# A diffusion step with SSD and differential attention on one core: prompt weights transposed in the other small PSUM bank, an output tile begun early, score blocks spaced anew

## The chip, the cores and the metric

One core of one Trainium2 chip. The metric is the device time of one execution in microseconds. The kernel before takes 1878.71 us, the median of three runs (1876.8 to 1879.6).

## What is computed

One inference step of a backbone with two layers. Layer 0 mixes tokens with a bidirectional Mamba-2 scan, layer 1 with differential attention; behind each stands a gated feed-forward part with a convolution of width 3. There are 128 context ("prompt") tokens and 512 latent tokens, the model is 1024 wide, and attention has 8 heads with two key maps of 64 each. The change touches attention and its output projection alone:

```python
def diff_attend(q, k, v, lam):
    ...
        s = jnp.einsum('bqhcd,bkhcd->bhcqk', qi, k, preferred_element_type=F32) * DA_SCALE
        p = jax.nn.softmax(s, axis=-1)
        w = p[:, :, 0] - lam * p[:, :, 1]
        return jnp.einsum('bhqk,bkhd->bqhd', w.astype(v.dtype), v)
...
def diff_out(o, subln_g, out_w, lam_init):
    b, l = o.shape[:2]
    o = (_rms(o) * subln_g.astype(F32) * (1.0 - lam_init)).astype(o.dtype)
    return o.reshape(b, l, D_MODEL) @ out_w
...
            op = diff_out(diff_attend(qp, kp, vp, lam), att_subln_g[slot], att_out_w[slot], lam_init)
            ...
            k_all = jnp.concatenate([cache_k[:, slot], ks_], axis=1)
            v_all = jnp.concatenate([cache_v[:, slot], vs], axis=1)
            os_ = diff_out(diff_attend(qs, k_all, v_all, lam), att_subln_g[slot], att_out_w[slot], lam_init)
```

Prompt tokens attend to prompt tokens. Latent tokens attend to 640 keys: 512 latent ones and 128 from the cache.

## The kernel before

Everything is float32 by three products: each operand is split into a high part and the rest (names ending in h and l, `whi` and `wlo` for weights), and a product is hi by hi, hi by lo and lo by hi. A **dense tile** is 128 output rows for all 640 tokens. Its 8 steps over the input (`dense_many`, L158) have six matmuls each, 256 and 384 columns for each of the three products. After each step comes `hook` (L76), which counts a **tick**. It also advances the generator tasks that are due: a task that says `yield n` gets its next turn n ticks later, and `drain` runs a task to its end. So the order in which the work is written down comes from the waits in these generators. A scheduler then sets the order on each engine from it, by what each instruction needs.

Attention (`attention`, L1169) makes for each head the tiles q, k and v. Beside them run these tasks. A head's prompt scores lie in its own v; its four score blocks and its tail lie beside the tiles of the next two heads:

- `att_head` (L1068): the prompt's scores (`sp`), then four blocks of 128 latent queries. A block's scores are two accumulators (`sl`), one for each key map. The vector engine takes the row maximum (`TENSOR_REDUCE`), the scalar engine the exponential `e` with its row sum, and both combine the two maps to the weights `w` (the prompt's are `wp`).
- `att_tail` (L1123): transposes the prompt's weights (`wpt`, copied to `wpT`), then, for five chunks of 128 keys, transposes four blocks of weights (`wt`), splits them on the scalar (`wTh`) and the vector engine (`wTl`) and multiplies by the values (`ov`, three matmuls). Then `op` for the prompt, the mean square (`osq`, `ms`), a reciprocal root in nine small steps on the vector engine (`rs_v`, `rs_a`, `rs_y`, L178 and following), and the scaling of `o`. Heads 0 to 6 spread the root over the partitions by way of DRAM (`rsd`, `rbc`), head 7 by matmuls (`obc`).
- `att_v` (L999): splits v and transposes it (`vt`).

Behind head 7's v come the output tiles (`po`): `project_out` (L282) multiplies heads 0 to 5 into tiles 0 to 4, and `project_last` (L290) adds heads 6 and 7 to these and makes tiles 5 to 7 from all eight heads, first for columns A (256 tokens), then B (384). `gate_add` adds a tile to the residual `xr`.

PSUM: dense tiles, `sp` and each `sl` take one of three slots of two banks. Two single banks remain. Bank "m" serves `vt`, `wt`, `wpt`, `op` and `ms` in turn, bank "y" serves `ov` and the norms' spreading. Weights are loaded and cast by units (`prefetch`, `cast`, `nextw`): `whi` by the scalar engine, `wlo` by the vector engine, three buffers each, so that the cast of a unit waits for the last use of the one three before.

## Time and profile before

| | |
|---|---|
| median of three runs | 1878.71 us |
| the profiled execution, its own time | 1880.65 us |
| its span | 1878.9 us |
| tensor engine busy | 98% of the span |
| vector engine busy | 73% |
| scalar engine busy | 51% |
| HBM | 111 GB/s |

The profile comes from one execution with the hardware profiler. Its span runs from the first to the last instruction; the execution's own time has 1.75 us more around it. Times in the trace count from the start of the span. Attention's heads with their tails lie between 1052 and 1353, the rest of the output projection up to 1400. PE is the tensor engine's matmuls, PEld its weight loads, DVE the vector and ACT the scalar engine. A wait is idle time of an engine, put down to the instruction whose end came last.

### The profile page before, as it was taken

The numbers are of one execution on the slowest core, as the hardware profiler recorded it, in microseconds if no ns is written. First come the engines' busy times: TensorE is split into PE (matmuls) and PEld (weight loads), VectorE is DVE, ScalarE is ACT, GpSimd is POOL, SyncE is SP. The second block draws the span as 40 slices with busy tenths as digits, with TensorE's granted clock in tenths as the row PEclk, the third lists the DMA queues.
The fourth block names the chain that finished last, engine by engine and source line by source line (L and its number), as shares of the span: only waits on it lengthen the run. The fifth ranks groups of instructions, "written<-read, shape, count | busy, mean of one in ns | idle before, by whom it ended". The sixth has DMA issues, their size and how long they took to land.

```text
span 1878.9 us, 32832 instructions
## 1 busy us (share of the span) xinstructions
PE 1838.2 (98%) x13322; PEld 1741.9 (93%) x13322; DVE 1369.5 (73%) x2637; ACT 952.9 (51%) x1745; POOL 0.2 (0%) x4
## 2 busy tenths in 40 slices
PE   7999999999999999999999999999999999999997
PEld 5899999999999999999999988888899999999996
DVE  5699999999658999974555877788777543553554
ACT  3489687878336441441443656566445432431441
POOL 0000000000000000000000000000000000000000
PEclk9999999999999999999999999999999999999998
DMA  9835243436624556532222212111122222122211
GB/s 337 266 121 147 97 147 109 140 115 202 199 80 142 185 180 221 181 103 91 68 68 78 79 40 65 58 50 48 61 88 89 69 79 80 63 72 89 64 40 57
DMA packets 79679, 209.74 MB, mean 112 GB/s; under 512 B 9276, under 2 KB 16040, under 8 KB 79400
## 3 DMA queue, kind: packets, MB, share of 16 engines
q1 hardware_dynamic: 78952, 207.13, 33.5%
q8 instruction: 104, 1.70, 0.4%
q10 hardware_dynamic: 576, 0.52, 0.1%
q14 instruction: 47, 0.39, 0.1%
HBM read 201.66 MB, written 5.96 MB: 111 GB/s over the span
## 4 chain that ended last, share of the span: by engine, by line
PE 91%; DVE 4%; ACT 3%; DMA 1%; issue 1%; SPq 0%; DVEq 0%; ACTq 0%
PE up L104 31%; PE po L104 25%; PE z L104 6%; PE x L104 5%; PE st L104 5%; PE bc L104 3%; PE yp L104 3%; PE q L104 2%; PE v L104 2%; PE k L104 1%; PE modrow L104 1%; PE sl L104 1%; PE in L104 1%; ACT whi L95 1%; ACT e L95 1%; PE ov L104 1%
## 5 line engine op out<-in xcount | busy, mean ns | idle before, releaser
L95 ACT ACTIVATE whi<-raw 128x1024 fp32r<-128x1024 f32 (+3 forms) x227 | 234.2, 1033 | 387.2 <-PE po L104 239.6
L101 DVE TENSOR_TENSOR wlo<-raw,whi 128x1024 fp32r<-128x1024 f32 (+2 forms) x226 | 269.2, 1192 | 172.2 <-ACT whi L95 165.1
L98 DVE SCALAR_TENSOR_TENSOR xr<-po,mod,xr 128x256 f32<-128x256 f32 (+2 forms) x231 | 89.2, 433 | 162.0 <-PE po L104 161.8
L104 PE MATMUL po<-mh,whi 128*128 128x256 f32 (+1 forms) x704 | 167.8, 310 | 0.0
L104 PE MATMUL po<-ml,whi 128*128 128x256 f32 (+1 forms) x704 | 167.5, 310 | 0.0
L104 PE MATMUL po<-mh,wlo 128*128 128x256 f32 (+1 forms) x704 | 167.3, 310 | 0.0
L104 PE MATMUL up<-h11h,wlo 128*128 128x256 f32 (+1 forms) x656 | 149.4, 309 | 0.0
L104 PE MATMUL up<-h01h,wlo 128*128 128x256 f32 (+1 forms) x656 | 149.4, 308 | 0.0
L104 PE MATMUL up<-h01h,whi 128*128 128x256 f32 (+1 forms) x656 | 149.3, 308 | 0.0
L104 PE MATMUL up<-h01l,whi 128*128 128x256 f32 (+1 forms) x656 | 149.3, 308 | 0.0
L104 PE MATMUL up<-h11l,whi 128*128 128x256 f32 (+1 forms) x656 | 149.3, 308 | 0.0
L104 PE MATMUL up<-h11h,whi 128*128 128x256 f32 (+1 forms) x656 | 149.3, 308 | 0.0
L104 PEld LDWEIGHTS po<-mh,whi 128*128 128x128 f32 x704 | 128.5, 188 | 0.7 <-ACT mh L95 0.5
L104 PEld LDWEIGHTS po<-mh,wlo 128*128 128x128 f32 x704 | 128.8, 188 | 0.0
L104 PEld LDWEIGHTS po<-ml,whi 128*128 128x128 f32 x704 | 128.6, 188 | 0.0
L104 PEld LDWEIGHTS up<-h01h,whi 128*128 128x128 f32 x656 | 119.3, 188 | 0.0
L104 PEld LDWEIGHTS up<-h01h,wlo 128*128 128x128 f32 x656 | 119.3, 188 | 0.0
L104 PEld LDWEIGHTS up<-h01l,whi 128*128 128x128 f32 x656 | 119.3, 188 | 0.0
L104 PEld LDWEIGHTS up<-h11h,whi 128*128 128x128 f32 x656 | 119.2, 188 | 0.0
L104 PEld LDWEIGHTS up<-h11h,wlo 128*128 128x128 f32 x656 | 119.2, 188 | 0.1
L104 PEld LDWEIGHTS up<-h11l,whi 128*128 128x128 f32 x656 | 119.2, 188 | 0.0
L98 DVE SCALAR_TENSOR_TENSOR ca<-uraw,fcw,ca 128x511 f32<-128x511 f32 (+1 forms) x176 | 85.2, 546 | 11.6 <-ACT ca L95 11.6
(497 smaller groups left out, 4315.6 us busy)
## 6 DMA issues: line engine op xcount, KB each, us to landing
raw<-in_w_up SPq DMA_DIRECT2D x88, 512.0 KB, 3.5
mw<-in_modT SPq DMA_DIRECT2D x48, 512.0 KB, 3.5
raw<-in_w_in SPq DMA_DIRECT2D x40, 512.0 KB, 5.5
rb<-rowd SPq DMA_DIRECT2D x40, 512.0 KB, 5.6
raw<-in_w_dn SPq DMA_DIRECT2D x32, 448.0 KB, 3.2
raw<-in_w_qkv SPq DMA_DIRECT2D x24, 512.0 KB, 3.5
mr<-in_mod SPq DMA_DIRECT2D x44, 256.0 KB, 5.7
mp<-in_modp SPq DMA_DIRECT2D x32, 256.0 KB, 5.4
```

What stands on the lines that cost most here:

```text
L95: return self.nc.scalar.activation(out, in_, func, **k)
L98: return self.nc.vector.scalar_tensor_tensor(out, in0, s, in1, op0, op1)
L101: return self.nc.vector.tensor_tensor(out, a, b, op)
L104: return self.nc.tensor.matmul(out, lhsT, rhs, start=start, stop=stop)
```

## The change

1. `dense_many`: a part of a tile's steps can be made alone (the last step is counted from `i0`).
2. `project_out` casts, at its last tile, one more unit of weights.
3. `project_last`: heads 0 to 5 of tile 5, columns A (18 matmuls) are made first, ahead of what heads 6 and 7 add to tiles 0 to 4; in the tile's old place only heads 6 and 7 are left (6 matmuls).
4. `weight_units`: the unit of tile 5 comes before the units with the weights of heads 6 and 7.
5. `att_head`: other waits between the prompt's scores and the four blocks, and between the blocks of heads 0 and 1; the task starts three ticks earlier for heads 1 to 6. In dense matmuls from one block to the next, the steady heads had 45, 27, 36 and 36, and have 39, 33, 36 and 36.
6. `att_tail`: `wpt` goes to bank "y"; the last key chunk waits three ticks, not two (head 7 stays at one).

```diff
--- before.py
+++ after.py
@@ -158,7 +158,7 @@
     def dense_many(self, tiles, ks, h, parts, n=None, i0=0):
 
 
-        n = n or len(ks)
+        n = n or i0 + len(ks)
         for i, k in enumerate(ks, i0):
             for ps, (hi, lo), m in tiles:
                 st, sp = i == 0, i == n - 1
@@ -279,11 +279,14 @@
         for a, b, c in COND[half]:
             self.stt(self.x[i][:, a:b], ps[:, COL0[half] + a:COL0[half] + b], g[:, i, c:c + 1], self.x[i][:, a:b], ALU.mult, ALU.add)
 
-    def project_out(self, h, ks, g, tiles=range(KT)):
+    def project_out(self, h, ks, g, tiles=range(KT), ahead=0):
 
         for i in tiles:
             ps = self.dense_ps("po")
-            self.dense(ps, self.nextw(), ks, h)
+            w = self.nextw()
+            if i == tiles[-1]:
+                self.cast(self.wi + ahead)
+            self.dense(ps, w, ks, h)
             for hf in "AB":
                 self.gate_add(i, ps, g, hf)
 
@@ -291,6 +294,8 @@
 
 
         self.norm_begin()
+        first = [(self.dense_ps("po"), self.nextw(), P)] if ks_last else []
+        self.dense_many(first, range(ks[0]), h, "A", KT)
         for i in range(KT - 3):
             ps = self.dense_ps("po")
             n = len(ks) * P
@@ -301,13 +306,14 @@
             for hf in "AB":
                 self.gate_add(i, ps, g, hf)
                 self.norm_sq(i, hf)
-        ks = ks_last or ks
+        ks_from, ks = ks[0], ks_last or ks
         if self.modtask:
             self.drain(self.modtask)
-        ws = [(self.dense_ps("po"), self.nextw(), i) for i in range(KT - 3, KT)]
+        ws = [(*(first[i] if i < len(first) else (self.dense_ps("po"), self.nextw()))[:2], KT - 3 + i) for i in range(3)]
         for hf in parts:
             for grp in ((ws[0:1], ws[1:3]) if hf == "B" else (ws[0:1], ws[1:2], ws[2:3])):
-                self.dense_many([(ps, w, P) for ps, w, i in grp], ks, h, hf)
+                i0 = ks_from if first and hf == "A" and grp == ws[0:1] else 0
+                self.dense_many([(ps, w, P) for ps, w, i in grp], ks[i0:], h, hf, i0=i0)
                 for ps, w, i in grp:
                     self.gate_add(i, ps, g, hf)
                     self.norm_sq(i, hf)
@@ -1098,7 +1104,7 @@
         last = hd == 7
         w = pool.tile([P, TP], F32, tag="wp", name="wp", bufs=1)
         combine(w, TP, *em, st)
-        yield 3 if last else 5 if hd else 3
+        yield {0: 3, 1: 13, 7: 3}.get(hd, 8)
         ws = []
         for b in range(4):
             qb = slice(b * P, (b + 1) * P)
@@ -1117,14 +1123,14 @@
             combine(wb, T, *em, st)
             ws.append(wb)
             if b < 3:
-                yield {0: (3, 2, 2), 6: (2, 2, 2), 7: (1, 1, 1)}.get(hd, (4, 4, 4))[b]
+                yield {0: (2, 3, 5), 1: (3, 3, 3), 6: (2, 2, 2), 7: (1, 1, 1)}.get(hd, (4, 4, 4))[b]
         self.tails[hd] = self.add(self.att_tail(hd, w, ws, vs, o, pool), 1 if last else 4)
 
     def att_tail(self, hd, w, ws, vs, os_, pool):
 
         nc = self.nc
         vh, vl, vp = vs
-        pm = self.bank("m", "wpt")
+        pm = self.bank("y", "wpt")
         nc.tensor.transpose(pm[:, :P], w, self.ident)
         wpT = pool.tile([P, TP], F32, tag="wpT", name="wpT", bufs=1)
         self.act(wpT, pm[:, :P], AF.Copy)
@@ -1150,7 +1156,7 @@
             if prev:
                 av(kc - 1, *prev)
             prev = hi, lo, gate
-            yield 1 if hd == 7 else 2
+            yield 1 if hd == 7 else 2 if kc < NCH - 1 else 3
         av(NCH - 1, *prev)
         self.act(o[:, :TS], py, AF.Copy)
         pm = self.psm.tile([P, 512], F32, tag="m", name="op")
@@ -1182,7 +1188,7 @@
             q = self.att_q(q, hd, pool)
             k = self.att_k(k, hd, pool)
             vs = []
-            tk.append(self.add(self.att_head(hd, qp, kp, q, k, vs, o, pool), 1 if hd == 7 else 4))
+            tk.append(self.add(self.att_head(hd, qp, kp, q, k, vs, o, pool), 1 if hd else 4))
             self.add(self.att_v(self.next_tile(h, "v"), hd, vs, pool), 1)
             if hd:
                 self.drain(tk[hd - 1])
@@ -1190,7 +1196,7 @@
         for i in range(n0):
             self.drain(self.tails[i])
         hy = [self.split(o[i], f"o{i}") for i in range(n0)]
-        self.project_out(hy, range(n0), self.gate(1, 0), range(KT - 3))
+        self.project_out(hy, range(n0), self.gate(1, 0), range(KT - 3), 1)
         self.drain(tk[7])
         for t in self.tails.values():
             self.drain(t)
@@ -1239,7 +1245,8 @@
         per = 1024 // (D - c)
         u += [(a["w_ao"][i:j, :, c:].rearrange("i p c -> p i c"), (j - i) * (D - c))
               for i in range(0, KT - 3, per) for j in (min(i + per, KT - 3),)]
-        u += [(a["w_ao"][i], D) for i in range(KT - 3, KT)]
+        u.insert(-2, (a["w_ao"][KT - 3], D))
+        u += [(a["w_ao"][i], D) for i in range(KT - 2, KT)]
         u += ffn(1)
         return u
```

No instruction is added or removed, but some stand elsewhere. Three places follow. Names carry no numbers there, except where the program numbers a buffer of its own. Lines of the changed file are 6 higher in this part, so L1134 is L1128 of before.

**First place: the tensor engine in head 2's v, from the last products of head 1's last score block to the first matmul of head 3's q.** Before:

```order
L104 MATMUL sl<-kh_11898,ql_11888 128x320 x4
L104 MATMUL v<-h10l_11229,whi_12157 128x384
L104 MATMUL v<-h10h_11228,wlo_12158 128x256
L104 MATMUL v<-h10h_11228,wlo_12158 128x384
L104 MATMUL v<-h10h_11230,whi_12157 128x256
L104 MATMUL v<-h10h_11230,whi_12157 128x384
L104 MATMUL v<-h10l_11231,whi_12157 128x256
L104 MATMUL v<-h10l_11231,whi_12157 128x384
L104 MATMUL v<-h10h_11230,wlo_12158 128x256
L104 MATMUL v<-h10h_11230,wlo_12158 128x384
L1128 MATMUL wpt<-cst,wp 128x128
L104 MATMUL q<-h10h_11216,whi_12330 128x256
```
and with the change:

```order
L104 MATMUL sl<-kh_11898,ql_11888 128x320 x4
L104 MATMUL v<-h10h_11230,whi_12152 128x256
L104 MATMUL v<-h10h_11230,whi_12152 128x384
L104 MATMUL v<-h10l_11231,whi_12152 128x256
L104 MATMUL v<-h10l_11231,whi_12152 128x384
L104 MATMUL v<-h10h_11230,wlo_12153 128x256
L104 MATMUL v<-h10h_11230,wlo_12153 128x384
L1134 MATMUL wpt<-cst,wp 128x128
L104 MATMUL q<-h10h_11216,whi_12307 128x256
```
Between the block and q stood nine matmuls of v and `wpt`; there are now six and `wpt`. On the scalar engine, the cast of the next weights, which waits for v's last use of its buffer, stands ahead of the `e` of this block.

**Second place: the tensor engine at the end of head 6's k, from head 5's third score block to v.** Before:

```order
L104 MATMUL sl<-kh_13601,ql_13591 128x320 x4
L104 MATMUL k<-h10h_11230,whi_13730 128x256
L104 MATMUL k<-h10h_11230,whi_13730 128x384
L104 MATMUL k<-h10l_11231,whi_13730 128x256
L104 MATMUL k<-h10l_11231,whi_13730 128x384
L104 MATMUL k<-h10h_11230,wlo_13731 128x256
L104 MATMUL k<-h10h_11230,wlo_13731 128x384
L104 MATMUL ms<-osq,cst 32x160 x4
L1128 MATMUL wpt<-cst,wp 128x128
L104 MATMUL v<-h10h_11216,whi_13873 128x256
```
With the change `wpt` has left this place. It stands behind the next score block but one, in head 7's q:

```order
L104 MATMUL q<-h10h_11220,wlo_14035 128x384
L104 MATMUL sl<-kh_14027,qh_14016 128x320 x4
L104 MATMUL sl<-kl_14028,qh_14016 128x320 x4
L104 MATMUL sl<-kh_14027,ql_14017 128x320 x4
L1134 MATMUL wpt<-cst,wp 128x128
L1021 MATMUL vt<-cst,v_14166 128x128 x4
L104 MATMUL q<-h10h_11222,whi_14034 128x256
```
From there, in a steady head, 24 or more matmuls of q, transposes of v and four `wt` follow before the first `ov`, which writes the bank that `wpt` uses. Between the block and v now stand the last three `ov`, `op` and six matmuls of k. On the vector engine, around the score block in v of the head before this one (`kl` and the two reduces; `wp` are the prompt's weights); before:

```order
L98 SCALAR_TENSOR_TENSOR w_13618<-e_13565,sm,e_13568 128x640
L1079 TENSOR_REDUCE sm<-sp 128x1
L101 TENSOR_TENSOR kl_13602<-k,kh_13601 128x640
L101 TENSOR_TENSOR rs_a<-rs_a,rs_y 128x160
L1087 RECIPROCAL sm<-sm 128x2
L98 SCALAR_TENSOR_TENSOR rs_a<-rs_a 128x160
L101 TENSOR_TENSOR sm<-sm,nlam 128x1
L98 SCALAR_TENSOR_TENSOR rs_y<-rs_a,rs_y 128x160
L98 SCALAR_TENSOR_TENSOR wp<-e_13666,sm,e_13669 128x128
L1079 TENSOR_REDUCE sm<-sl 128x1 x2
```
With the change:

```order
L101 TENSOR_TENSOR k<-k,ru 128x512
L98 SCALAR_TENSOR_TENSOR w_13618<-e_13558,sm,e_13561 128x640
L178 TENSOR_SCALAR rs_v<-ms 128x160
L101 TENSOR_TENSOR kl_13602<-k,kh_13601 128x640
L1085 TENSOR_REDUCE sm<-sl 128x1 x2
L179 TENSOR_SCALAR rs_y<-rs_v 128x160
L1093 RECIPROCAL sm<-sm 128x2
```
The reduces stand directly behind `kl` now; five steps of the root and `wp`, which stood between, come after them.

**Third place: the vector engine around head 7's reciprocal root, up to the scaling of o by obc.** Before:

```order
L98 SCALAR_TENSOR_TENSOR rs_y<-rs_a,rs_y 128x160
L101 TENSOR_TENSOR rs_a<-rs_v,rs_y 128x160
L101 TENSOR_TENSOR rs_a<-rs_a,rs_y 128x160
L98 SCALAR_TENSOR_TENSOR xr_5178<-po,mod_113,xr_5178 128x256
L98 SCALAR_TENSOR_TENSOR rs_a<-rs_a 128x160
L98 SCALAR_TENSOR_TENSOR xr_5178<-po,mod_113,xr_5178 128x256
L98 SCALAR_TENSOR_TENSOR rs_y<-rs_a,rs_y 128x160
L98 SCALAR_TENSOR_TENSOR xr_5178<-po,mod_113,xr_5178 128x128
L101 TENSOR_TENSOR wlo_15158<-raw_15030,whi_15157 128x256
L98 SCALAR_TENSOR_TENSOR o_14907<-o_14907,sg,obc 128x640
```
With the change:

```order
L98 SCALAR_TENSOR_TENSOR rs_y<-rs_a,rs_y 128x160
L98 SCALAR_TENSOR_TENSOR xr_5178<-po,mod_113,xr_5178 128x256
L101 TENSOR_TENSOR rs_a<-rs_v,rs_y 128x160
L98 SCALAR_TENSOR_TENSOR xr_5178<-po,mod_113,xr_5178 128x128
L101 TENSOR_TENSOR rs_a<-rs_a,rs_y 128x160
L101 TENSOR_TENSOR wlo_15107<-raw_15030,whi_15106 128x1024
L98 SCALAR_TENSOR_TENSOR rs_a<-rs_a 128x160
L98 SCALAR_TENSOR_TENSOR rs_y<-rs_a,rs_y 128x160
L98 SCALAR_TENSOR_TENSOR o_14886<-o_14886,sg,obc 128x640
```
A `wlo` of 1024 columns and all three `xr` of a tile now stand within the root's chain; before, two `xr` stood in it, and a `wlo` of 256 columns behind it. On the tensor engine, 14 matmuls of po stood between `ms` and `obc`, and 8 stand there now.

## Rows read from the trace of the kernel before

**Rows 1.** The page's part 1: busy time, share of the span and instructions of each engine.
```profile
PE 1838.2 (98%) x13322; PEld 1741.9 (93%) x13322; DVE 1369.5 (73%) x2637; ACT 952.9 (51%) x1745; POOL 0.2 (0%) x4
```

**Rows 2.** Windows: length, busy time of each engine (instructions), granted clock, DMA share, GB/s.
```profile
583.00:1010.00 427.00, 427.00 (x2907) 426.81 (x2907) 329.14 (x563) 166.15 (x205) 0.00 (x0) 1.00 0.41 137
1186.26:1223.10 36.84, 35.32 (x248) 30.79 (x248) 28.68 (x58) 22.45 (x48) 0.00 (x0) 1.00 0.17 58
1400.00:1860.00 460.00, 459.63 (x3139) 458.79 (x3138) 236.81 (x403) 177.90 (x226) 0.00 (x0) 1.00 0.20 68
```

**Rows 3.** Waits of the tensor engine, 1052 to 1400: us in total, times, longest.
```profile
PE q L104 <- ACT e L95: 3.4, 6, 1.8
PE v L104 <- ACT e L95: 2.8, 6, 0.8
PE wpt L1128 <- DVE rs_v L178: 2.2, 5, 0.4
PE obc L104 <- DVE rs_y L98: 1.5, 1, 1.5
PE ov L104 <- DVE wTl L101: 1.3, 4, 0.3
PE sl L104 <- ACT e L95: 1.2, 1, 1.2
PE ms L104 <- ACT sq L95: 1.1, 1, 1.1
PE po L104 <- ACT e L95: 1.0, 2, 0.7
```

**Rows 4.** Timeline of all engines, 1216 to 1237: start, length, instruction, [idle before <-releaser].
```profile
1220.70 0.46 PE L104 MATMUL sl<-kh,ql 64*128 64x320 f32 x4
...
1221.98 1.06 ACT L95 ACTIVATE whi<-raw 128x1024 fp32r<-128x1024 f32 x1 [1.44 <-PE k L104]
...
1222.94 0.78 ACT L95 ACTIVATE e<-sl,sm 128x640 f32<-128x640 f32 x1
...
1223.10 0.33 PE L1128 MATMUL wpt<-cst,wp 128*128 128x128 f32 x1 [0.45 <-DVE rs_v L178]
...
1223.87 0.56 PE L104 MATMUL v<-h10h,whi 128*128 128x256 f32 x2 [0.45 <-ACT e L95]
```

**Rows 5.** Timeline, tensor engine, 1115 to 1131.
```profile
1120.35 0.46 PE L104 MATMUL sl<-kh,ql 64*128 64x320 f32 x4
1120.74 0.45 PE L104 MATMUL v<-h10l,whi 128*128 128x384 f32 x1
...
1122.71 0.56 PE L104 MATMUL q<-h10h,whi 128*128 128x256 f32 x2 [0.24 <-ACT e L95]
```

**Rows 6.** Timeline, tensor engine, 1080 to 1092.
```profile
1085.78 0.90 PE L104 MATMUL q<-h10h,whi 128*128 128x256 f32 x2 [1.83 <-ACT e L95]
...
1090.05 0.56 PE L104 MATMUL sl<-kh,qh 64*128 64x320 f32 x4
```

**Rows 7.** Windows, the stretch behind that wait; columns as in rows 2.
```profile
1085.78:1088.60 2.82, 2.82 (x10) 2.82 (x11) 1.08 (x3) 2.04 (x4) 0.00 (x0) 0.50 0.19 74
```

**Rows 8.** Timeline of all engines, 1341 to 1362.
```profile
1345.79 1.22 DVE L101 TENSOR_TENSOR wlo<-raw,whi 128x1024 fp32r<-128x1024 f32 x1
...
1347.55 0.48 PE L104 MATMUL ms<-osq,cst 128*32 128x160 f32 x8
...
1351.80 1.35 PE L104 MATMUL obc<-rs_y,cst 128*128 128x160 f32 x8 [1.52 <-DVE rs_y L98]
...
1353.29 0.46 PE L104 MATMUL po<-o0l,whi 128*128 128x256 f32 x2
...
1354.88 0.82 DVE L101 TENSOR_TENSOR o7l<-o,o7h 128x640 fp32r<-128x640 f32 x1 [0.81 <-ACT o7h L95]
...
1358.49 1.14 DVE L98 SCALAR_TENSOR_TENSOR xr<-po,mod,xr 128x256 f32<-128x256 f32 x3 [2.79 <-PE po L104]
...
1359.47 0.45 PE L104 MATMUL po<-o7l,whi 128*128 128x256 f32 x2
```

## Prediction

> **What bounds the kernel now.** I read the page's part 1 first: the tensor engine is busy 98% of the span, the vector engine 73%, the scalar engine 51% [rows 1]. So only two things can move the time: what the tensor engine computes, and the moments in which it waits. The change adds and removes no instruction; it moves them and gives one transpose another PSUM bank. What is left is waiting. The windows then show where there is any [rows 2]: a dense stretch (583 to 1010) has none, at 427.00 / 2907 = 0.147 us for a matmul of this kind, so 0.29 us for a pair of 256 and 384 columns; the stretch after attention has 0.4 us in 460; one steady attention head (1186.26 to 1223.10) has 36.84 - 35.32 = 1.52 us. Third, the waits of the tensor engine between 1052 and 1400, which is all that the change touches: the eight rows add up to 14.5 us [rows 3]. That is the whole stake, 0.8% of the time. It is made of many small waits for "ACT e" (a score block holds two of the three 2-bank PSUM slots until the scalar engine has read it, and the next dense tile q, k, v or po needs one of them), five of 0.45 us of wpt for the reader of bank m, and one of 1.5 us for obc.
>
> The Trainium skill (page "Perfetto Trace Analysis", section "Identifying the Most-Contended Engine") says that matmul busy time is no good measure of the distance to the roofline, and that the busy share of the weight loads is a better one. In the steady head that would leave 36.84 - 30.79 = 6.05 us where the gaps leave 1.52 [rows 2], and a better order might then win some 6 us a head, not 1.5. The trace doesn't bear it out for this change: the same matmuls are issued, and an order can only fill gaps between them. By the one the sum below could fall by some 24 us over heads 2 to 5, by the other by 6 at most; I keep to the gaps.
>
> **The price of a score block.** Everything below uses two prices. In [rows 4] the last products of a block start at 1220.70 and end, by the start of what follows, near 1221.09; the weight cast whi (1.06 us) stands ahead of e on the scalar engine, and the waiting v starts at 1223.87: **2.8 us** after the block. In [rows 5] no cast is ahead, the block ends by 1120.74, and q starts at 1122.71, **2.0 us** after it. A tile that claims a slot waits for one of these prices less the work that lies between on the tensor engine.
>
> **The change part by part.** A head's four blocks run beside the next head's tiles; below, a head is named by its blocks.
>
> *wpt in bank y.* Before, wpt directly follows ms in bank m and waits for rs_v to read it, 0.45 us in each of five heads [rows 3, 4]. In bank y the earlier user is the ov of the head before, read long ago. So 2.2 us of waits go. What is late next is v, which in [rows 4] waited 0.45 us more behind wpt, so part only moves. The copy of wpt must now be done before the bank's first ov; between the two stand some 24 matmuls of q (24 x 0.147 = 3.5 us), more than the 2.8 us in which the scalar engine gets through a cast and an e. I cost it at nothing; in head 7 the cover is 11 po matmuls, a wt and an ms, about 2.4 us, and there up to 1 us could show.
>
> *Heads 2 to 5.* The blocks were 45, 27, 36 and 36 dense matmuls apart and are now 39, 33, 36 and 36. Behind the block in k now stand three ov, op and six k matmuls, some 1.9 us, and the first e is ahead of the cast, so v waits 2.0 - 1.9 = 0.1 us. The q wait (3.4 - 1.8 = 1.6 us over the other five of the six, 0.3 each [rows 3]) stays: the block in v comes six matmuls earlier, but its reduces stand behind a w and kl in the vector engine's queue. The last ov no longer waits for wTl (0.3 us each [rows 3]) but two of the transposes wt come a little late behind vl and wTl in the vector engine's queue, some 0.25 each. So 0.1 + 0.3 + 0.5 = 0.9 us a head for 1.52, 0.6 less in each of four heads. Bounds a head: -1.52 (all gaps go) and 0. **-2.4 us.**
>
> *Head 0* is bound by the vector engine. It waits 1.2 us at sl [rows 3] and 1.83 us at q [rows 6], and behind that second wait the granted clock is 0.50, the lower of its levels, 1.2 GHz, for 2.8 us [rows 7], so that q's first 18 matmuls take from 1085.78 to 1090.05 [rows 6], 4.3 us, where 18 x 0.147 = 2.6. The new order takes the wait ahead of sl down, but the reduces of the fourth block then stand behind w and wlo, and q starts at about the same time, with a wait of over 3 us for 1.83. **0 us**; bounds -3 (both waits and the low clock gone) and +1.5.
>
> *Head 1* gets its first block 16 ticks after its start, where it was 11, and so two blocks fall into the next v. Behind the second stand only six v matmuls and wpt, 0.88 + 0.16 = 1.04 us, where nine stood [rows 5], and the next cast, which needs v's last use of its buffer, comes ahead of this block's e. So q waits 2.8 - 1.04 = 1.75 us, against 0.24: +1.5. The k tile of this stretch claims its slot behind a block that four wt and three ov follow, about 1.25 us: 0.7 to 1.5 us of wait where none was, I take 1.0. **+2.5 us**; bounds 0 (the cast never in the way, vector engine on time) and +3.5.
>
> *Head 6.* The k tile comes six q matmuls (0.88 us) behind a block, with a cast ahead of e: 1.1 to 1.9 us, less what waited there before, about 1 us in all. **+0.6 us.**
>
> *The tail.* The two po tiles that waited 1.0 us together [rows 3] follow their blocks by less work; 1.0 to 2.5, I take 2.0: **+1.0**. Then obc. From ms at 1347.55 the chain on the vector engine takes 4.25 us to obc at 1351.80, with two xr of the gate in it [rows 8]. In the new order three xr, one more at some 0.15 us net, and one wlo of 1024 columns stand in it; such a wlo keeps the engine from 1345.79 to the next start at 1346.92, 1.13 us [rows 8]. So 4.25 + 0.15 + 1.13 = about 5.5 us; I take 5.4, as in part the xr fall into the chain's own gaps. And between ms and obc the tensor engine has 8 matmuls (1.2 us) and ms itself (0.4) where it had 14 (2.1 us). So obc waits 5.4 - 1.6 = 3.8 us for 1.52: **+2.3 us.** Bounds: 0 (the wlo comes late enough not to stand in the chain, and the xr move) and +2.5.
>
> *Tile 5 begun ahead.* Its 18 matmuls of heads 0 to 5 now stand before the parts that need heads 6 and 7. They would hide a late o7; but o7l runs from 1354.88 for 0.82 us and its first reader starts at 1359.47 [rows 8], so they hide nothing: 0. That tile holds a PSUM slot meanwhile, so the five others turn in two, with 12 x 0.147 = 1.76 us a tile against 1.14 us for its three xr [rows 8]: 0 to +0.5. The weight unit that is cast a call earlier was loaded already, since each call loads three ahead; the swapped order of units moves three loads on SP's queue, at a DMA share of 0.17 [rows 2]: 0.
>
> **Sum:** -2.4 + 0 + 2.5 + 0.6 + 1.0 + 2.3 = **+4.0 us.** The profiled execution took 1880.65 us, 1.94 above the median of the runs, 1878.71. By it the changed kernel's would be 1884.7; against the median **1882.7 us**. A measurement of this kernel tells about 0.2% (3.8 us) from no change, and the forecast lies just beyond that.
>
> **Rivals.**
> 1. *Faster: the even spacing pays.* If the reduces of a block run within 1 us of its end and the casts fall behind e, the v and q waits of heads 2 to 5 go whole (-6), head 0's two waits shrink and the clock stays up (-3), and head 1 adds nothing; the tail's +2.3 stays: about 1872. For it: even gaps of 33 matmuls and more are 4.8 us, above both prices. Against: the vector engine is busy 28.68 of 36.84 us in a head [rows 2], and its queue is in order. It decides if the q waits of heads 2 to 5 fall under 0.1 us. Chance 0.20.
> 2. *The waits only change place.* The gains of heads 2 to 5 and the losses of head 1 and 6 cancel, and obc loses little because wlo's cast is late: 0 to +3, about 1880. Chance 0.34.
> 3. *The forecast:* +4 to +6, 1882.5 to 1885. Chance 0.35, the likeliest.
> 4. *Slower still: the clock.* Idle of 1.83 us, with 1.2 us shortly before, ended with half the clock [rows 6, 7]; 1.52 us ahead of obc alone did not: the po pairs behind it take 0.46 us [rows 8]. A wait of 3.8 us ahead of obc, or 1.75 in head 1, may do it, at 4.3 - 2.6 = 1.6 us each: about 1886, with both 1888. Chance 0.11.
> That tile 5's start doesn't do what it is for is in the forecast already.
>
> **Numbers.** The predicted time is that of the forecast, 1882.7. The range over all cases goes from 1873 (the greater part of rival 1, with head 0's full gain, left out) to 1889. Faster by over 0.2%: rival 1, 0.20; within: rival 2, 0.34; slower: forecast and rival 4, 0.46.
>
> **What would show it.** In the waits of the tensor engine: wpt gone; obc near 3.8 us; one q over 1.5 us behind head 1's last block, and a k near 1 us ahead of it; v of heads 3 to 5 near 0.1 us. A steady head of about 36.3 us. If obc's wait stays at 1.5, the tail was misjudged; if the steady heads fall under 36 us or head 0's q runs at full clock, rival 1 is right. The time of the stretches before 1052 and after 1400 must not change.

## The result and the profile after

The changed kernel takes **1884.13 us** (median of 12 runs, 1881.3 to 1888.3) where the kernel before takes 1879.43 in the same comparison (12 runs, 1876.8 to 1883.1): a ratio of 1.0027 with a 95% interval of 1.0018 to 1.0036, 4.7 us slower. The forecast was +4.0. The profiled execution took 1883.83 us, its span is 1882.0.

The page's part 1 shows what [rows 1] show; the change moves no share of any engine:

```profile
PE 1837.4 (98%) x13322; PEld 1744.8 (93%) x13322; DVE 1368.4 (73%) x2637; ACT 953.8 (51%) x1745; POOL 0.2 (0%) x4
```

The windows of the changed kernel (length, busy time and instructions of each engine, granted clock, DMA share, GB/s), the answer to [rows 2]. The dense stretches are untouched. In attention two heads (1162 to 1236) have lost their waits altogether, and the stretches before and behind them have more:

```profile
583.00:1010.00 427.00, 427.00 (x2914) 426.82 (x2913) 329.74 (x563) 165.88 (x204) 0.00 (x0) 1.00 0.43 135
1088.00:1125.00 37.00, 34.00 (x243) 29.92 (x242) 26.89 (x55) 22.45 (x47) 0.00 (x0) 1.00 0.14 44
1162.00:1199.00 37.00, 37.00 (x267) 33.19 (x266) 30.93 (x62) 24.07 (x52) 0.00 (x0) 1.00 0.22 63
1199.00:1236.00 37.00, 36.81 (x264) 32.82 (x263) 28.72 (x60) 23.86 (x51) 0.00 (x0) 1.00 0.21 71
1273.00:1310.00 37.00, 32.84 (x227) 27.93 (x224) 30.05 (x61) 23.82 (x51) 0.00 (x0) 1.00 0.10 31
1310.00:1353.00 43.00, 37.76 (x244) 33.01 (x244) 32.58 (x66) 21.81 (x40) 0.00 (x0) 0.96 0.17 57
1410.00:1860.00 450.00, 449.96 (x3069) 449.35 (x3069) 229.91 (x381) 174.07 (x218) 0.00 (x0) 1.00 0.22 67
```

The waits of the tensor engine between 1052 and 1405 (us in total, times, longest), to be laid beside [rows 3]. The five of wpt and the four of ov are gone, sl and v have shrunk; vt, o5h and wlo are new, k has grown from one wait of 0.28 to two of 1.41, and obc from 1.5 to 3.7:

```profile
PE q L104 <- ACT e L95: 4.8, 2, 3.3
PE obc L104 <- DVE rs_y L98: 3.7, 1, 3.7
PE vt L1027 <- DVE wTl L101: 3.4, 2, 1.8
PE k L104 <- ACT e L95: 2.8, 2, 1.4
PE po L104 <- ACT o5h L95: 1.3, 1, 1.3
PE po L104 <- ACT e L95: 1.2, 2, 0.9
PE v L104 <- ACT e L95: 1.0, 2, 0.7
PE po L104 <- DVE wlo L101: 1.0, 1, 1.0
```

**Where the 4.7 us come from.** I took the stretch from the first q matmul of the last attention part to the last wait of `st` (the first dense tiles of the feed-forward part behind attention), which bounds all that the change touches: 349.96 us before (from 1053.41), 355.05 after (from 1051.21), +5.09. The idle times in the tensor engine's rows of that stretch add up to 15.54 us in 30 gaps before and to 20.15 in 16 gaps after, +4.61. So there are about half as many waits, and their sum is 30% larger. The other 0.48 us are work that ran longer: two stretches of halved clock, from 1352.78 and from 1318.95, cost 1.56 and 1.25 us (each against the same pieces in the experiment e13_tail, where the clock stayed up), and some 2.3 us came back elsewhere. Of those, some 1.5 may be the piece behind a wait, which takes 0.40 us to the next start where others take 0.29; 14 gaps fewer at 0.11. That is an estimate and was not tried by itself.

Ten of the 16 gaps, from the timeline of the tensor engine of the changed kernel (obc's, 3.66 us, stands with e13_tail below); the number in brackets is the wait:

```profile
1083.82 0.90 PE L104 MATMUL q<-h10h,whi 128*128 128x256 f32 x2 [3.27 <-ACT e L95]
1098.72 0.56 PE L104 MATMUL k<-h10h,whi 128*128 128x256 f32 x2 [1.41 <-ACT e L95]
1123.03 0.56 PE L104 MATMUL q<-h10h,whi 128*128 128x256 f32 x2 [1.52 <-ACT e L95]
1148.62 0.56 PE L104 MATMUL v<-h10h,whi 128*128 128x256 f32 x2 [0.71 <-ACT e L95]
1239.22 0.33 PE L1027 MATMUL vt<-cst,v 128*128 128x128 f32 x1 [1.50 <-DVE wTl L101]
1275.25 0.33 PE L1027 MATMUL vt<-cst,v 128*128 128x128 f32 x1 [1.85 <-DVE wTl L101]
1279.67 0.39 PE L104 MATMUL k<-h10h,whi 128*128 128x256 f32 x1 [1.41 <-ACT e L95]
1318.07 0.56 PE L104 MATMUL po<-o5h,whi 128*128 128x256 f32 x2 [1.26 <-ACT o5h L95]
1318.95 0.90 PE L104 MATMUL po<-o0h,whi 128*128 128x256 f32 x2 [0.32 <-ACT e L95]
1374.06 0.38 PE L104 MATMUL po<-o0h,wlo 128*128 128x256 f32 x1 [1.02 <-DVE wlo L101]
```

**The two vt waits** were in no step of the prediction. The timeline of the vector engine ahead of the first of them (1226 to 1242) shows whom vt waits for. The vector engine stands idle for 2.11 us at the head's scaling `o<-o,sg,rbc`, until the root has come back from DRAM, and w and wTl of the next head stand behind the scaling in the engine's queue:

```profile
1229.29 0.33 DVE L98 SCALAR_TENSOR_TENSOR rs_y<-rs_a,rs_y 128x160 f32<-128x160 f32 x1
1229.57 0.89 DVE L98 SCALAR_TENSOR_TENSOR w<-e,sm,e 128x640 f32<-128x640 f32 x1
1230.51 1.23 DVE L101 TENSOR_TENSOR wlo<-raw,whi 128x1024 fp32r<-128x1024 f32 x1
...
1236.88 0.88 DVE L98 SCALAR_TENSOR_TENSOR o<-o,sg,rbc 128x640 f32<-128x640 f32 x1 [2.11 <-DMA rbc<-rsd]
1237.68 0.88 DVE L98 SCALAR_TENSOR_TENSOR w<-e,sm,e 128x640 f32<-128x640 f32 x1
1238.48 0.68 DVE L101 TENSOR_TENSOR wTl<-wt,wTh 128x512 fp32r<-128x512 f32 x1
```

The rows of SP's queue for the same stretch show what is new ahead of rbc: the load of the next weight unit, raw, has come between the two transfers of the root.

```profile
1229.64 0.50 SPq L215 DMA_DIRECT2D rsd<-rs_y  x1
1231.77 0.33 SPq L125 DMA_DIRECT2D raw<-in_w_ao  x1
1232.19 1.09 SPq L217 DMA_DIRECT2D rbc<-rsd  x1
```

raw goes out at 1231.77, as wlo, which stands at 1230.51 for 1.23 us and reads a raw buffer, ends (1231.74), and rbc goes out behind it. Before, the same two transfers of this head stood next to each other, 1.58 us apart instead of 2.55:

```profile
1231.13 0.50 SPq L215 DMA_DIRECT2D rsd<-rs_y  x1
1232.71 0.33 SPq L217 DMA_DIRECT2D rbc<-rsd  x1
```

Before, the scaling of this head waited 0.24 us. So rbc goes out 1 us later behind rsd, and from its issue to the scaling's start pass 4.69 us (1232.19 to 1236.88) where 3.36 did (1232.71 to 1236.07). With the old spacing (before, e3_tile5) raw comes behind rbc in this place, with the new one (the change, e2_space, e4_notile5, e5_hold, e6_head1, e13_tail, e16_three) between the two. The order on SP's queue doesn't make a wait by itself, though: one head earlier raw stands between the two transfers as well (1196.87), and the scaling at 1201.64 waits for nothing; and the first head's scaling, at 1125.47, waits 1.33 us though its two transfers stand next to each other (1120.21 and 1121.80).

### The profile page after: what moved, and what is told of

It reads as the page before. It is cut to its first block, busy times and chain, and to the rows that moved or that the text cites. A ratio compares the mean times of both kernels' runs of the same rounds, so it can differ in the third digit from the quotient of the medians.

```text
span 1882.0 us, 32842 instructions
## 1 busy us (share of the span) xinstructions
PE 1837.4 (98%) x13322; PEld 1744.8 (93%) x13322; DVE 1368.4 (73%) x2637; ACT 953.8 (51%) x1745; POOL 0.2 (0%) x4
## 4 chain that ended last, share of the span: by engine, by line
PE 91%; DVE 4%; ACT 3%; DMA 1%; issue 1%; SPq 0%; DVEq 0%; ACTq 0%
PE up L104 31%; PE po L104 25%; PE z L104 6%; PE x L104 5%; PE st L104 5%; PE bc L104 3%; PE yp L104 3%; PE k L104 2%; PE q L104 2%; PE v L104 2%; ACT e L95 1%; PE ov L104 1%; PE modrow L104 1%; PE sl L104 1%; PE in L104 1%; PE wt L1151 1%
## 5 line engine op out<-in xcount | busy, mean ns | idle before, releaser
L95 ACT ACTIVATE whi<-raw 128x1024 fp32r<-128x1024 f32 (+4 forms) x227 | 234.2, 1033 | 388.2 <-PE po L104 240.4
```

The costliest lines, as they stand in the source:

```text
L95: return self.nc.scalar.activation(out, in_, func, **k)
```

## The experiments

Each was timed in up to five rounds, 5 to 12 executions, against the kernel before on the same chip. The ratio is to the kernel before, with its 95% interval; stretch and idle are measured as above, in the profiled execution. Most intervals reach some 1.7 us to either side, so the times alone tell a difference between two of the experiments to about 2.4 us; what is read of smaller ones rests on the rows of one profiled execution each.

| kernel | ratio | stretch, us | idle in it, us |
|---|---|---|---|
| before | 1 | 349.96 | 15.54 |
| the change | 1.0027 [1.0018, 1.0036] | 355.05 | 20.15 |
| e1_bank | 0.9993 [0.9984, 1.0002] | 348.55 | 13.77 |
| e2_space | 1.0042 [1.0030, 1.0055] | 360.22 | 21.35 |
| e3_tile5 | 1.0008 [0.9999, 1.0017] | 350.79 | 15.98 |
| e4_notile5 | 1.0008 [0.9999, 1.0017] | 350.95 | 17.36 |
| e5_hold | 1.0015 [1.0006, 1.0023] | 351.87 | 16.62 |
| e6_head1 | 1.0009 [1.0000, 1.0018] | 353.52 | 17.28 |
| e13_tail | 1.0010 [1.0002, 1.0019] | 350.89 | 17.50 |
| e16_three | 0.9966 [0.9953, 0.9979] | 343.65 | 11.61 |
| e11_e9hold | 0.9996 [0.9988, 1.0005] | 349.15 | 13.21 |
| e10_mix | 0.9988 [0.9979, 0.9996] | 347.71 | 12.87 |
| e15_heads1to4 | 0.9964 [0.9952, 0.9976] | 343.37 | 10.46 |
| e17_head0 | 0.9953 [0.9940, 0.9967] | 340.88 | 9.04 |

### The change's parts alone

**e1_bank**, the kernel before with the bank alone:

```
-        pm = self.bank("m", "wpt")
+        pm = self.bank("y", "wpt")
```

> The kernel before with the prompt weights' transpose in bank y and nothing else. Theory (waits only move when the bank alone is changed): in heads 1 to 5 wpt keeps its place behind ms, its wait of 0.45 us goes, and v behind it waits 0.9 us instead of 0.45, since its slot comes free when it did; in the tail 22 matmuls now stand between ms and obc and no wlo or xr inside the root's chain, so obc waits near 0 instead of 1.5 us. About 1.5 us less than before: 1877.9 us. Rival (the wpt waits are a real gain): 2.2 us more, 1875.7. Rival (nothing): 1879.4.

1878.26 us, 1.0 below the kernel before and inside what can be told from no change. The wpt row is gone, and each steady head's v takes over the whole of it: 0.96 us where wpt and v had 0.45 and 0.44. The order of the tail also moves, though: 22 output-projection matmuls now stand between ms and obc, and obc waits for nothing. So by the rows the bank is worth what it frees in the tail, not what it frees at wpt.

**e2_space**, the spacing alone (the four edits of the diff in att_head, att_tail and attention, without the bank):

```
-        yield 3 if last else 5 if hd else 3
+        yield {0: 3, 1: 13, 7: 3}.get(hd, 8)
```

> The kernel before with the new spacing alone (the waits in att_head, its start, the last key chunk). Theory (the loss is in the spacing): q behind head 0 waits over 3 us, q and k of head 1 1.4 us each, vt 1.5 to 1.8 us in heads 4 and 5 behind the vector engine's wait for rbc, heads 2 and 3 without waits; obc 2.5 us or more. 3 to 4 us more than before: about 1883. Rival (the loss is the early tile 5's): within 1 us of before.

1886.76 us, +7.9 by the ratio: the direction was right and the size half of what it is. Both vt waits are longer (1.89 and 2.35 us). The two scalings wait longer too (2.35 and 2.28 us), and with wpt in bank m it and the value transposes vt turn in one bank; which of the two counts was not tried. The clock is also at half in more places (granted 0.83 in 1240 to 1250 and in 1276 to 1286).

**e3_tile5**, the early sixth tile with its unit order and its cast, and the old bank and spacing (the changed kernel with those edits taken back):

```
-        pm = self.bank("y", "wpt")
+        pm = self.bank("m", "wpt")
...
-        yield {0: 3, 1: 13, 7: 3}.get(hd, 8)
+        yield 3 if last else 5 if hd else 3
```

> The kernel before with tile 5 begun ahead, its unit of weights before the others and the earlier cast; spacing and bank as before. Theory: obc waits 1.5 us as before, since the wlo of 1024 columns stands behind the root's chain here; the wait of 1.0 us for a late wlo in tile 6 shows, the last ms waits 0.8 us less. Plus 0.2 us: 1879.7. Rival (the loss is the early tile's): 2 to 3 us more, 1882.

1881.38 us, +1.5 by the ratio, whose interval just reaches 1; the time lies between the two theories, nearer to the rival. The output projection's wait for wlo, 1.02 us, is there, the last ms waits 0.64 for 1.13, and obc keeps its 1.51.

**e4_notile5**, the change without the sixth tile: bank and spacing together, with project_out, project_last and the unit order of before.

```
-        u.insert(-2, (a["w_ao"][KT - 3], D))
-        u += [(a["w_ao"][i], D) for i in range(KT - 2, KT)]
+        u += [(a["w_ao"][i], D) for i in range(KT - 3, KT)]
```

> The changed kernel without the early tile 5 (its unit order and cast undone too): bank and spacing alone. Theory: obc's chain holds a wlo of 256 columns (0.4 us) instead of 1024 (1.2), so obc waits 2.9 us instead of 3.7; the wait for wlo in tile 6 (1.0) goes, the last ms waits 1.1 instead of 0.4. About 1 us under the changed kernel: 1883. Rival (the early tile is the loss): 1880.

1880.89 us, +1.5 by the ratio; here the rival's number came out. The waits at q 3.28, k 1.41, q 1.52, k 1.41 are all there, obc waits 2.86 and the clock stays up behind it, and there is no wait for wlo. The last ms waits 0.31, not the 1.1 expected. The first of the two vt waits is 0.60 where the changed kernel has 1.50: raw stands between rsd and rbc here too (1230.13, 1232.26, 1232.68), and the scaling waits 1.21 for 2.11.

So the parts don't add: -1.3 (bank) +7.9 (spacing) +1.5 (tile) would be +8.1, and the change is +5.1 by its ratio. Most of what the spacing loses the bank takes back; the early tile then adds 3.6 us (1.0027 against 1.0008), of which the wait for wlo (1.02), 0.8 more at obc, 0.9 more at the first vt, and halved clock behind obc can be seen. The intervals of the two ratios leave it between some 1 and 6 us.

### Undoing one suspected loss in the changed kernel

**e5_hold**: the scaling of heads 0 to 4 stands behind the next head's wTl in the vector engine's queue. It is written three ticks later (12 for 9) and held behind the last wTl; the two were not tried apart.

```
-            bc = yield from self.rms_spread(pool, [sq], P, 9)
-        self.stt(o, o, self.sg[:, hd // 7:hd // 7 + 1], bc[:, :T], ALU.mult, ALU.mult)
+            bc = yield from self.rms_spread(pool, [sq], P, 12 if hd < 5 else 9)
+        i = self.stt(o, o, self.sg[:, hd // 7:hd // 7 + 1], bc[:, :T], ALU.mult, ALU.mult)
+        if hd < 5:
+            self.hold(i, [self.last])
```

> The changed kernel with one thing more: in heads 0 to 4 the scaling of a head's output by its root, o<-o,sg,rbc, is made to stand behind the next head's w and wTl on the vector engine, so that nothing of the next head queues behind it while it waits for the root's round trip through DRAM. Theory (the vector engine stands 2.1 us at that scaling, and the weight parts wTl behind it come late to the transposes vt of heads 4 and 5): the two vt waits, 1.50 and 1.85 us, fall under 0.4 each, the wait of po for o5h (1.26) stays, obc stays near 3.7; time about 1881, 3 us under the changed kernel. Rival (the vector engine is late by its own work and the wait at the scaling only fills a hole that it has anyway): the vt waits stay above 1 us each and the time stays within 1 us of 1884. Second rival: the vt waits go but come back at the next e or q: time the same, with q or k of heads 4 to 6 waiting over 1 us.

1881.73 us, ratio 1.0015. The two vt waits of 1.50 and 1.85 are down to one of 0.26 (wt waits 0.5 in all instead), and the k of head 6, 1.41, went to 0.28 as well, which I had not expected: what stood behind the waiting scaling had held that up too. The vector engine's timeline shows the scaling with no wait at all, behind w and wTl:

```profile
1239.46 0.89 DVE L98 SCALAR_TENSOR_TENSOR w<-e,sm,e 128x640 f32<-128x640 f32 x1 [0.96 <-ACT e L95]
1240.26 0.68 DVE L101 TENSOR_TENSOR wTl<-wt,wTh 128x512 fp32r<-128x512 f32 x1
1240.98 0.89 DVE L98 SCALAR_TENSOR_TENSOR o<-o,sg,rbc 128x640 f32<-128x640 f32 x1
```

Idle falls by 3.5 us, though raw still stands between rsd and rbc. The order of the operations on the vector engine's queue, not the amount of work, was the loss.

**e6_head1**: head 1 by the rule of heads 2 to 5.

```
-        yield {0: 3, 1: 13, 7: 3}.get(hd, 8)
+        yield {0: 3, 7: 3}.get(hd, 8)
...
-                yield {0: (2, 3, 5), 1: (3, 3, 3), 6: (2, 2, 2), 7: (1, 1, 1)}.get(hd, (4, 4, 4))[b]
+                yield {0: (2, 3, 5), 6: (2, 2, 2), 7: (1, 1, 1)}.get(hd, (4, 4, 4))[b]
```

> The changed kernel with head 1's score blocks placed by the rule of heads 2 to 5 (first block 8 steps after its w, then 4, 4, 4) in place of its own (13, then 3, 3, 3). Theory of the prediction (head 1's q and k wait because two of its blocks fall into the next v and the last of them stands six matmuls ahead of wpt and q): the q wait of 1.52 and the k wait of 1.41 at heads 1 and 2 both fall under 0.4; time 2.0 to 2.9 us under the changed kernel, about 1881.5. Rival (the vector engine is behind here after head 0, whatever the spacing of head 1): k or q of this stretch still wait over 1 us each, or the head after it waits in v or vt, and the time stays within 1 us of 1884.

1879.79 us, 3.4 below the changed kernel by the ratios. Both waits, k 1.41 and q 1.52, are gone; what is left in the whole stretch from 1090 to 1238 is one v of 0.71, as in the changed kernel. So head 1's own placing is the cause, as predicted; that the weight cast stands ahead of e there is in the rows of the scalar engine (whi at 1121.15, e at 1122.11, q at 1123.03).

**e13_tail**: the three xr and the 1024-column wlo that stood within the last head's root are held behind the root's last operation.

```
+        if self.guard:
+            self.root, self.guard = i, False
...
+                if self.root and u > self.wi:
+                    self.hold(y, [self.root])
...
+            if self.root:
+                self.hold(y, [self.root])
```

(in rsqrt, where i is its last operation and guard is set for the last head alone; in cast, for the unit cast a call early; in gate_add.)

> The changed kernel with the last head's root kept together: the three gate additions xr of the tile before last and the 1024-column weight part wlo are made to stand behind the root's last operation in the vector engine's queue. Theory (the prediction's chain: obc waits 3.66 us because a 1024-column wlo and three xr stand among the nine operations of the root): from the root's start to its end the chain takes about 3.2 us and not 4.9, obc waits 1.9 to 2.2 us, the clock stays at its upper level behind it, and the time falls by 1.7 to 2.5 us to about 1882. Rival (the root's operations are spaced by their own latency, and xr and wlo fill the holes): obc still waits over 3 us, the time within 0.7 us of 1884. Second rival (the held xr or wlo are then late themselves): the wait of po for wlo, 1.02 us, grows, or a po tile waits behind obc, and the time stays.

1882.28 us, ratio 1.0010, 3.2 below the changed kernel. obc waits 1.85 us for 3.66 and the clock stays up:

```profile
1349.47 0.48 PE L104 MATMUL ms<-osq,cst 128*32 128x160 f32 x8
...
1353.18 1.35 PE L104 MATMUL obc<-rs_y,cst 128*128 128x160 f32 x8 [1.85 <-DVE rs_y L98]
```

The same two in the changed kernel, with the wlo inside the chain and obc, at half clock, taking 2.24 us for 1.35:

```profile
1347.26 0.48 PE L104 MATMUL ms<-osq,cst 128*32 128x160 f32 x8
...
1350.91 1.21 DVE L101 TENSOR_TENSOR wlo<-raw,whi 128x1024 fp32r<-128x1024 f32 x1
...
1352.78 2.24 PE L104 MATMUL obc<-rs_y,cst 128*128 128x160 f32 x8 [3.66 <-DVE rs_y L98]
```

From ms to obc the chain takes 3.71 us alone and 5.52 with the four guests, 1.81 more, which is the 1.81 that obc waits less.

**e16_three**: the diffs of e5_hold, e6_head1 and e13_tail at once.

> The changed kernel with three repairs at once: head 1 placed by the rule of heads 2 to 5, the scaling held behind the next head's wTl, and the last head's root kept together. If the waits that were named are the change's loss and do not come back elsewhere, the gains add: 3.4 us (head 1 alone) + 2.3 (scaling alone) + 1.7 to 2.5 (root) under the changed kernel's 1884.1, about 1876.5, and under the kernel before by 2. Rival (the parts don't add, as with the change's own three parts, since one stall hides another): 1879 to 1881.

1873.74 us, ratio 0.9966: 11.5 us under the changed kernel (0.0061 of 1880) and 6.4 under the kernel before, more than the sum of the single gains. The idle times do add: 3.5 + 2.9 + 2.7 = 9.1 of the single runs against 20.15 - 11.61 = 8.5 here. The other 2.9 us are work that ran shorter, 332.04 for 334.90; from 1100 on the granted clock is 1.00 here and was 0.99 in the three single repairs and in the changed kernel. So what was named is the change's loss, and without it the change would gain.

### A version that beats both

**e11_e9hold**: before, with wpt in bank y, heads 1 to 6 spaced by the new rule, head 0 as before, no early tile, and the scaling held as in e5_hold. Against before:

```
-        yield 3 if last else 5 if hd else 3
+        yield {0: 3, 7: 3}.get(hd, 8)
...
-            yield 1 if hd == 7 else 2
+            yield 1 if hd == 7 else 2 if kc < NCH - 1 else 3
...
-            tk.append(self.add(self.att_head(hd, qp, kp, q, k, vs, o, pool), 1 if hd == 7 else 4))
+            tk.append(self.add(self.att_head(hd, qp, kp, q, k, vs, o, pool), 1 if hd else 4))
```

> A version put together from the parts that helped: the kernel before with wpt in the other bank, heads 1 to 6 spaced as the changed kernel spaces heads 2 to 6, head 0 spaced as before, no early sixth tile, and the scaling held behind the next head's wTl. Theory (the parts' losses are head 0's q 3.3, head 1's q and k, the two vt and the tail's obc): no vt wait over 0.4, no q over 2 in head 0, obc near 2.9 as with the bank and the spacing alone; time about 1876, 3 under the kernel before. Rival (a loss that is taken away comes back at the next claim of a slot, since the scores and the vector engine have no slack left): 1879 to 1881, no better than the kernel before.

1877.63 us, ratio 0.9996: not the 3 us hoped for. vt waits 0.25 and obc 2.86 as expected, but head 0 now waits 1.70 at sl and 3.10 at q (before 1.20 and 1.83) beside a head 1 that is placed by the new rule, and half clock follows the waits of the tail (granted clock 0.95 in 1300 to 1335 and in 1335 to 1370).

**e10_mix**: as e11_e9hold, with heads 1 and 6 placed as before as well (their start and, for head 6, the last key chunk too).

```
-        yield {0: 3, 7: 3}.get(hd, 8)
+        yield {0: 3, 1: 5, 6: 5, 7: 3}.get(hd, 8)
```

> As the put-together version, but with heads 1 and 6 placed as in the kernel before too (first block 5 steps after w at head priority 4), so that heads 2 to 5 alone are respaced and the end of attention is nearly that of the kernel before. Theory (the obc wait comes from where the last head's work ends up behind head 6's spacing, as five matmuls and not eight stand between ms and obc here, but no 1024-column weight part stands in the vector engine's chain): obc 1.5 to 2.5, heads 2 to 5 nearly free of waits; time 1874 to 1877. Rival: head 6's k and the po tiles wait as much as they gain, 1879 to 1881.

1876.57 us, ratio 0.9988, 2.3 us under the kernel before. obc waits 3.22, not 1.5 to 2.5: the tail hardly changed. That part of the theory fell: it isn't head 6's placing alone that sets how much work stands ahead of obc.

**e15_heads1to4**: as e11_e9hold, but heads 0, 5 and 6 as in the kernel before, so that heads 1 to 4 alone are respaced.

```
-        yield 3 if last else 5 if hd else 3
+        yield {0: 3, 5: 5, 6: 5, 7: 3}.get(hd, 8)
...
-            yield 1 if hd == 7 else 2
+            yield 1 if hd == 7 else 2 if kc < NCH - 1 or hd in (5, 6) else 3
...
-            tk.append(self.add(self.att_head(hd, qp, kp, q, k, vs, o, pool), 1 if hd == 7 else 4))
+            tk.append(self.add(self.att_head(hd, qp, kp, q, k, vs, o, pool), 4 if hd in (0, 5, 6) else 1))
```

> As the put-together version with only heads 1 to 4 respaced: heads 0, 5 and 6 are placed as in the kernel before, wpt in the other bank, the scaling held, no early sixth tile, so that 22 matmuls stand between ms and obc as with the bank alone. Theory (the tail's losses, obc 3.2, po for o5h 1.25 and their half clock, come from the respacing of heads 5 and 6 alone): no wait at obc, none for o5h, one v of 0.9 back in head 5; time 1873 to 1875, 4 to 5 us under the kernel before. Rival (po and wpt wait in the tail as much instead): 1876 to 1878, no better than with heads 2 to 5 alone.

1873.0 us, ratio 0.9964. With head 5 back the tail is that of e1_bank, 22 matmuls between ms and obc: no wait at obc and none for o5h; the price is one po of 1.46. In e10_mix, with head 6 as before and head 5 respaced, 5 matmuls stood there, obc waited 3.22 and o5h 1.25; e11_e9hold, with head 1 respaced as here, has both waits too. So both go with head 5's spacing.

**e17_head0**: as e15_heads1to4, with the change's own blocks in head 0:

```
-                yield {0: (3, 2, 2), 6: (2, 2, 2), 7: (1, 1, 1)}.get(hd, (4, 4, 4))[b]
+                yield {0: (2, 3, 5), 6: (2, 2, 2), 7: (1, 1, 1)}.get(hd, (4, 4, 4))[b]
```

> As the version with heads 1 to 4 respaced (0.9964 of the kernel before), with one thing more: head 0's blocks as the changed kernel places them (2, 3, 5 in place of 3, 2, 2). Theory (the part of the change in head 0 is itself good: its waits are sl 0.37, v 0.33 and q 3.3 where the unchanged blocks beside a respaced head 1 wait v 0.78, sl 1.70 and q 3.10): 1.6 us less, 1871.5 where the kernel before stands at 1880.3, a ratio near 0.9955. Rival (head 0 is bound by the vector engine, so that what is taken from sl and v comes back at q or k): ratio 0.996 to 0.997, and q over 4 us or a k wait behind it.

**1872.02 us**, ratio 0.9953 with an interval of 0.9940 to 0.9967: by the ratio 8.8 us under the kernel before, and the fastest of the study; the interval overlaps that of e15_heads1to4, but the gain was in sl and v, where it was expected (0.36 and 0.34 for 1.70 and 0.78). The first of its waits in 1052 to 1402:

```profile
PE q L104 <- ACT e L95: 3.8, 3, 3.3
PE po L104 <- ACT e L95: 1.8, 2, 1.5
PE v L104 <- ACT e L95: 1.1, 2, 0.7
PE wt L1145 <- DVE wTl L101: 0.5, 2, 0.3
PE ms L104 <- ACT sq L95: 0.4, 1, 0.4
```

Of the change this version keeps the bank, head 0 and the spacing of heads 2 to 4; it leaves out its head 1, heads 5 and 6 and the early tile, and takes the scaling out of the way.

## Why the prediction was right, and which of its steps failed

The sum was +4.0; the idle times give +4.62 by the same parts, and the median +4.7.

| part | forecast | measured, from the rows of both traces |
|---|---|---|
| head 0 | 0 | 4.01 before, 3.97 after: -0.04 |
| head 1 | +2.5 | k 1.41, q 1.52 for 0.42 (q and wt): +2.51 |
| heads 2 to 5 | -2.4 | 6.20 before; v 0.71, vt 1.50 and 1.85 after: -2.14 |
| head 6 | +0.6 | k 1.41 for k, wpt and v 0.96 before: +0.45 |
| po tiles | +1.0 | po 1.17 and o5h 1.26 for 0.98: +1.45 |
| obc | +2.3 | 3.66 for 1.52: +2.14 |
| early tile | 0 to +0.5 | wlo +1.02, last ms 0.36 for 1.13: +0.25 |

- **obc** was right in mechanism and size, 3.66 us for 3.8. e13_tail shows the cause that was named: the 1024-column wlo and the xr within the root.
- **Head 1** was right in both places: q 1.52 (net 1.28) for 1.75 (net 1.5), k 1.41 for 1.0; e6_head1 shows that its own placing is the cause.
- **Head 0** was right: the wait moved from sl and v to q (3.27 us, "over 3"), and the half clock stayed. The rows show the cause that was named, the reduces at 1082.03 directly behind w (1079.94) and wlo (1080.89); it was not tried by itself. Beside a head 1 placed by the new rule its blocks are better by the rows, 10.46 - 9.04 = 1.42 us of idle between e15_heads1to4 and e17_head0; the 2.1 us between their ratios lie within the intervals.
- **Heads 2 to 5** are right by number and wrong by mechanism. The step that failed is that the q wait "stays", since the reduces "stand behind a w and kl in the vector engine's queue", with the two transposes wt that were to come "some 0.25 each" late. No q or wt wait is left in any of them, the sign by which rival 1 was to be told, and two heads turn with no wait at all. On SP's queue the rsd of successive heads come 36.83 and 36.82 us apart before and 35.44, 34.90 and 36.23 after; that rival's steady heads under 36 us are there in two of three. What ate the gain was the vt wait, 3.35 us, which stood in no term: I counted each queue for the early tile and not SP's queue for the root, where a weight load now comes between rsd and rbc. e5_hold shows that these waits come from the scaling that waits for the root's round trip ahead of other work; that raw makes the round trip late was read from the rows and not tried by itself, and it can't be all, as the scalings at 1201.64 and 1125.47 show.
- **The early tile.** Its term said "0 to +0.5", its own rows give +0.25, and its 18 matmuls hid nothing: o7l ends at 1357.56 in the changed kernel, the first matmul of o6 starts at 1363.00. The step that put the weight units at 0, as "loaded already", was wrong. The unit of tile 6 has its cast at 1370.00, when the tensor engine lets go of a buffer, and its wlo then stands behind gate additions until 1372.79, 1.02 us too late for the tensor engine:

```profile
1370.00 1.06 ACT L95 ACTIVATE whi<-raw 128x1024 fp32r<-128x1024 f32 x1 [0.58 <-PE po L104]
1372.79 1.22 DVE L101 TENSOR_TENSOR wlo<-raw,whi 128x1024 fp32r<-128x1024 f32 x1
```

With 0.8 at obc and the clock the tile costs more than its own rows show, 3.6 us by the difference of two ratios.
- **The clock** (rival 4, 0.11) came in part. Behind obc the granted clock is 0.54 from 1352.78 to 1356.41, the lower level with a few pieces at 2.4 GHz behind it, and the same pieces take 3.63 us for 2.07 in e13_tail: 1.56, as priced (1.6). It came also at 1318.95, behind waits of 1.26 and 0.32, which no rival had. That the sum still held is luck in part: 2.8 us of clock against some 2.3 that came back elsewhere.
- The Trainium skill's measure (page "Perfetto Trace Analysis", section "Identifying the Most-Contended Engine") would have left some 6 us a head to win by the weight loads' busy share. The trace bears out the gaps: where all of them went (1162 to 1199) a head takes 34.9 to 35.4 us for 36.8, 1.4 to 1.9 less, against gaps of 1.52 [rows 2], and with no wait left the loads there are busy 33.19 of 37.00 us.

So of the seven terms three were right: head 1 and obc with a cause that was tried, head 0 with one read from the rows. Two were near in size with another cause in part: head 6's k goes to 0.28 in e5_hold, so the waiting scaling holds it up too, and of the po tiles' 1.45 us o5h makes up 1.26 and the claim of a slot, which the +1.0 was for, 0.19. In heads 2 to 5 two errors nearly cancelled, 2.9 us of waits that I kept and that went (0.71 left of 3.6), and 3.35 us of vt that I didn't see. The range of 1873 to 1889 holds the time.

Still open: what makes rbc late; how much the early tile costs (1 to 6 us by the times; 2.8 us of idle by the rows of one execution each, 0.9 of it at a vt that its own steps don't touch); and the 2.3 us by which the work between the gaps ran shorter.

## What to carry to other kernels

When a change moves steps, follow every queue that they are moved past, the transfer queue too: here a weight load slipped between the two halves of a DRAM round trip, the vector engine stood at the reader of that round trip, and the tensor engine waited 3.4 us for the work behind it. Such a reader was cheap to move: put behind the next work that the engine had anyway, it waited for nothing (e5_hold). And try the parts of a scheduling change apart, then take out what they collide with: the new spacing alone lost 7.9 us, the whole change with three repairs gained 6.4 (e16_three), and a part of the spacing with the bank and one of the repairs 8.8 (e17_head0).

## What the runs showed of the hardware that I had not expected

The same wait is followed by half a clock for different times. After 3.27 us of idle ahead of head 0's q, the changed kernel has a granted clock of 0.53 for the next 3.2 us and 1.00 behind; e5_hold, with the same wait of 3.27 and the same instructions, is still at the lower of the two levels (1.2 GHz) four microseconds on. Windows of the changed kernel, then of e5_hold:

```profile
1083.82:1087.04 3.22, 3.22 (x13) 3.22 (x13) 1.23 (x4) 2.04 (x4) 0.00 (x0) 0.53 0.33 130
1087.04:1091.00 3.96, 3.96 (x29) 3.70 (x29) 0.69 (x1) 0.88 (x2) 0.00 (x0) 1.00 0.00 0
```

```profile
1088.00:1090.00 2.00, 2.00 (x9) 2.00 (x9) 0.77 (x1) 0.00 (x0) 0.00 (x0) 0.50 0.00 0
1090.00:1092.00 2.00, 2.00 (x10) 1.93 (x10) 0.00 (x0) 0.13 (x1) 0.00 (x0) 0.53 0.00 0
1092.00:1094.00 2.00, 2.00 (x16) 1.91 (x14) 0.69 (x1) 0.65 (x2) 0.00 (x0) 1.00 0.00 0
```

Of the 14 kernels' profiled executions the clock of 1083 to 1100 is 0.90 in seven and 0.80 in seven, and waits of 3.27 and 3.28 us ahead of that q are in both groups. The waits for o5h and e at 1318 (1.26 and 0.32 us) were followed by half clock in the changed kernel and not in e13_tail (1.25 and 0.33). A wait of 2.86 us at obc was followed by full clock in e4_notile5 (1.00 from 1351.70 to 1355) and by 0.72 from 1348.70 to 1352 in e11_e9hold. So waits of this length were followed by half clock in some executions and not in others, and a single profile doesn't tell their price to better than some 1.5 us here.
